# A transformer block's output projection and MLP: a scheduler's order replaced by the order of the source

## The chip, the core and the metric

The kernel runs on one core of a Trainium2 chip. A core has TensorE (PE, matrix products and transposes; its weight loads are listed apart as PEld), VectorE (DVE), ScalarE (ACT), GpSimd (POOL) and SyncE (SP), which here only issues DMA transfers. Each engine works through its own queue in order and waits on semaphores for the others. The metric is the time of one execution on the device in microseconds (us).

## The reference

One layer of a hybrid decoder block on x of 1024 rows by 1024 columns, float32. Two branches (sparse attention and a state-space scan) are merged; the part that matters here is its end:

```
merged = sigmoid(g_a) * y_a + sigmoid(g_b) * y_b
x  = x + merged @ w_out                           # 1024 x 1024
h2 = rmsnorm(x, norm_mlp_g)
x  = x + square(relu(h2 @ w_up)) @ w_down         # 1024 x 4096 and 4096 x 1024
return rmsnorm(x, norm_final_g)
```

rmsnorm(x, g) is x / sqrt(mean(x*x) + 1e-6) * g, per row.

## The kernel before

Every float32 product is made of three matmuls. An operand is split into a high part in fp32r (a cast on ScalarE) and a low part, the rest (a subtraction on VectorE or GpSimd), and high x high, low x high and high x low are added up in PSUM. So a product of a 128x512 weight block with four 128x512 blocks of the other operand is 12 matmuls.

The two products of the MLP are done by a fast scheme with seven products of half size in place of eight. With h2 cut into B11, B21 (rows 0 to 511, the two halves of the columns) and B12, B22 (rows 512 to 1023), the operands on the side of the rows are B11, B21, B22, T1 = B12 - B11, T2 = B22 - T1, T3 = B22 - B12 and T4 = B21 - T2. The weights' sums are formed per unit.

**Output projection (line 118 to 120, tile ps_o; 1033).** Two column halves, each of eight row blocks of 128 rows, 24 matmuls a block. After the second half of a row block is added to x (L1033), `norm2` norms the row: square with sum (L124), the power on GpSimd (L127), the scale and gain in one VectorE pass over 1024 columns (L977), eight transposes on PE into two PSUM banks (L983), a copy to SBUF (`hb`, L984). Rows 0 to 3 are split to B11 and B21 (L968, L969); for rows 4 to 7 the transposed blocks are subtracted (T1 in two steps from the two parts of B11, L998; T2, L1001), then split. T3 and T4 are formed later over whole operands from the split parts of others (`late_operand`, L1009 to 1014).

**Up products (L1043, tiles pa, pb, pc).** Sixteen units q; each has weights of two 128x1024 rows of w_up and seven products of 12 matmuls: two in `up_open` (B11, B21), two in `up_mid` (T2, T1), three in `up_end` (T3, B22, T4). Sums of the weights are VectorE subtractions and additions (L1070 to 1073), then a cast (L111) and a split on GpSimd (L112). Products are copied or added on ScalarE and VectorE (L1060, L1062, L1078, L1080, L1089, L1092), squared after the ReLU (L1047, L1048), summed to seven operands and written to DRAM in pairs of units (act_d, L1103 to L1105). Even units' weights are loaded by L105, odd ones by L1112, all on SyncE, where the writes are issued too.

**Down products (L1146, tile pg).** Seven operands by 16 steps of 12 matmuls. Each step takes 128x512 of the seven stored operands (loaded on SyncE, two steps at a time, L1152, two buffers) and 128x512 of w_down (loaded on ScalarE's queue by `fetch`, L1215, six steps ahead), with its own cast and split (L1164 to 1167). Then come adds to x, final norm and the write.

What sets the order: the source calls these helpers one after another, and a scheduler then lays out every engine's queue by its own estimate of when an instruction can run.

## Time and profile before

| | us |
|---|---|
| median of 3 runs (1648.69 to 1650.01) | 1648.78 |
| the profiled execution | 1651.35 |
| its span in the trace | 1649.5 |
| PE busy | 1536.3 (93%) |
| PE weight loads busy | 1281.3 (78%) |
| VectorE busy | 1038.6 (63%) |
| ScalarE busy | 744.4 (45%) |
| GpSimd busy | 471.7 (29%) |

The mean granted clock of TensorE is 0.967 of full speed. The span begins at the first instruction; what the execution takes beyond its span lies outside the trace. Busy shares are means over the whole span: the branches take the first half, the output projection lies at about 807 to 900 us, the up products follow to 1302.5, and the down products and the tail fill the rest.

### The profile page before, as it was taken

To read this page: it belongs to the slowest core of one execution; us is meant where nothing else is said; L and a number is where in the kernel's file an instruction comes from. 1 tells how busy PE (TensorE), PEld (TensorE's weight loads), DVE (VectorE), ACT (ScalarE), POOL (GpSimd) and SP (SyncE) were. 2 spreads that over 40 slices of the span, in tenths; PEclk is the share of its full clock that TensorE was granted. 3 is DMA by queue.
4 is the path that set the end of the run, shared out by engine and by line. 5 is a ranking of instruction groups with operands and counts; after the bars stand their busy time and mean duration, and the time that the engine had idled before them with its cause. 6 is when DMAs were issued, how large, how long until landed. Compare 5 with 4: busy or idle time off the path is not lost.

```text
span 1649.5 us, 22305 instructions
## 1 busy us (share of the span) xinstructions
PE 1536.3 (93%) x7890; PEld 1281.3 (78%) x7890; DVE 1038.6 (63%) x1871; ACT 744.4 (45%) x1555; POOL 471.7 (29%) x438
## 2 busy tenths in 40 slices
PE   7999999999999999999999586889899949999997
PEld 6789899888888888888888465777777738788886
DVE  7995967378889785754514883344343349755675
ACT  6344443357667675422204453444444323344453
POOL 3133544210001000000003433343324335444453
PEclk9999999999999999999999797999999979999999
DMA  6345465721132112733412123333343793344343
GB/s 225 122 117 171 117 190 149 223 75 57 60 101 64 55 49 97 254 104 127 179 51 102 64 80 111 134 140 141 141 140 115 250 327 93 90 142 151 94 130 109
DMA packets 113647, 212.12 MB, mean 129 GB/s; under 512 B 14720, under 2 KB 49536, under 8 KB 113536
## 3 DMA queue, kind: packets, MB, share of 16 engines
q1 hardware_dynamic: 104320, 193.92, 35.9%
q10 hardware_dynamic: 9216, 16.78, 2.8%
q8 instruction: 62, 1.02, 0.2%
q14 instruction: 49, 0.40, 0.1%
HBM read 140.41 MB, written 68.16 MB: 126 GB/s over the span
## 4 chain that ended last, share of the span: by engine, by line
PE 77%; DVE 10%; DMA 5%; issue 2%; ACT 2%; POOL 1%; SPq 0%; POOLq 0%; DVEq 0%; ACTq 0%
PE pg L1146 18%; PE ps_m L150 10%; PE pa L1043 9%; PE s_ps L763 4%; PE pt L804 3%; PE pc L1043 3%; PE ps_v L120 3%; PE ps_v L118 3%; PE ps_v L119 3%; PE o_ps L714 2%; PE pb L1043 2%; PE o_ps L715 2%; DMA raw<-w_up 2%; PE ps_o L120 2%; PE ps_o L118 2%
## 5 line engine op out<-in xcount | busy, mean ns | idle before, releaser
L1146 PE MATMUL pg<-w 128*128 128x512 f32 x1344 | 313.6, 394 | 23.7 <-ACT w L1164 20.8
L1146 PEld LDWEIGHTS pg<-w 128*128 128x128 f32 x1344 | 253.7, 190 | 83.4 <-ACT w L1164 21.3
L112 POOL TENSOR_TENSOR w<-raw,w 128x1024 fp32r<-128x1024 f32 (+2 forms) x75 | 179.0, 2398 | 334.1 <-ACT w L111 297.4
L150 PE MATMUL ps_m<-hT,w 128*128 128x512 f32 x768 | 215.1, 400 | 0.4 <-ACT mst L156 0.3
L1165 POOL TENSOR_TENSOR w<-raw,w 128x512 fp32r<-128x512 f32 x112 | 156.1, 1396 | 183.4 <-ACT w L1164 181.0
L1164 ACT CAST w<-raw 128x512 fp32r<-128x512 f32 x112 | 69.1, 620 | 190.7 <-POOL w L1165 111.5
L150 PEld LDWEIGHTS ps_m<-hT,w 128*128 128x128 f32 x768 | 130.6, 189 | 21.4 <-ACT mst L156 0.8
L1043 PE MATMUL pa<-T,w 128*128 128x512 f32 x576 | 140.8, 394 | 3.8 <-ACT T L1013 2.2
L1043 PEld LDWEIGHTS pa<-T,w 128*128 128x128 f32 x576 | 108.1, 188 | 30.1 <-ACT T L1013 2.6
L111 ACT CAST w<-raw 128x1024 fp32r<-128x1024 f32 (+2 forms) x98 | 95.0, 979 | 65.1 <-DMA raw<-w_out 16.6
L1167 DVE TENSOR_TENSOR w<-xy,w 128x512 fp32r<-128x512 f32 x64 | 70.9, 1118 | 65.2 <-ACT w L1166 41.5
L1043 PE MATMUL pa<-B,w 128*128 128x512 f32 x192 | 66.3, 495 | 39.4 <-ACT w L111 27.3
L769 ACT ACTIVATE p<-s_ps,sst 128x640 f32<-128x640 f32 (+7 forms) x128 | 90.2, 708 | 23.5 <-PE pt L804 13.4
L1043 PEld LDWEIGHTS pa<-B,w 128*128 128x128 f32 x192 | 45.8, 243 | 57.0 <-ACT w L111 30.3
L127 POOL TENSOR_TENSOR rstd<-ss,neghalf 128x1 f32<-128x1 f32 x16 | 9.3, 580 | 281.2 <-DVE ss L125 281.2
L763 PE MATMUL s_ps<-kT,qT 128*128 128x512 f32 (+3 forms) x384 | 85.9, 337 | 0.3
L804 PE MATMUL pt<-ident,p 128*128 128x128 f32 x528 | 83.8, 275 | 2.1 <-DVE pl__5079 L708 1.0
L1167 DVE TENSOR_TENSOR w<-z,w 128x512 fp32r<-128x512 f32 x48 | 60.6, 1268 | 39.3 <-ACT w L1166 39.3
L766 DVE CUSTOM_DVE_ANT_0 s_ps<-s_ps,cmask 128x256 f32<-128x256 f32 (+7 forms) x96 | 63.9, 677 | 19.9 <-PE s_ps L763 19.4
L119 PE MATMUL ps_a<-w,hT 128*128 128x256 f32 (+1 forms) x256 | 74.7, 292 | 0.0
L118 PE MATMUL ps_a<-w,hT 128*128 128x256 f32 (+1 forms) x256 | 74.5, 291 | 0.0
L120 PE MATMUL ps_a<-w,hT 128*128 128x256 f32 (+1 forms) x256 | 73.9, 289 | 0.0
(1423 smaller groups left out, 3458.2 us busy)
## 6 DMA issues: line engine op xcount, KB each, us to landing
raw<-act_d SPq DMA_DIRECT2D x56, 512.0 KB
raw<-w_up SPq DMA_DIRECT2D x35, 512.0 KB
act_d<-ts SPq DMA_DIRECT2D x16, 1024.0 KB
raw<-w_mg SPq DMA_DIRECT2D x16, 512.0 KB
mg_d<-mst SPq DMA_DIRECT2D x32, 256.0 KB
act_d<-e SPq DMA_DIRECT2D x16, 512.0 KB
xy<-w_down ACTq DMA_DIRECT2D x32, 256.0 KB
z<-w_down ACTq DMA_DIRECT2D x32, 256.0 KB
```

What stands on the lines that cost most here:

```text
L111: (hi or A.copy)(w[:, 0, :], raw)
L112: (lo or V.tensor_tensor)(w[:, 1, :], raw, f32(w[:, 0, :]), op=ALU.subtract)
L118: T.matmul(ps, lhsT=wh, rhs=xh, start=first and i == 0, stop=False)
L119: T.matmul(ps, lhsT=wl, rhs=xh, start=False, stop=False)
L120: T.matmul(ps, lhsT=wh, rhs=xl, start=False, stop=last and i == n - 1)
L150: m = T.matmul(ps, lhsT=w[:, e, ks], rhs=hT[k][:, r, hs], start=k == 0 and i == 0, stop=k == KD - 1 and i == 2)
L763: T.matmul(s_ps[:, o:o + hi - lo], lhsT=qT[:, 2 + hp * 2 + j, :], rhs=kT[g, br, hf][:, e, lo - hf * 512:hi - hf * 512], start=e == 0, stop ...
L804: T.transpose(pt[:, i, j, :], c[hp, br][j][:, (i0 + i) * P:(i0 + i + 1) * P], ident)
L1043: T.matmul(ps, lhsT=w[:, e, ks], rhs=x[:, k], start=first and k + i == 0, stop=k == 3 and i == 2, skip_group_check=not first)
L1146: T.matmul(ps[b], lhsT=w[:, 0, e, bs], rhs=w[:, 1, r], start=first and q + i == 0, stop=q == 15 and i == 2, skip_group_check=not first)
L1165: G.tensor_tensor(w[:, 0, 1], raw[:, q % 2], f32(w[:, 0, 0]), op=ALU.subtract)
L1167: V.tensor_tensor(w[:, 1, 1], t, f32(w[:, 1, 0]), op=ALU.subtract)
```

## The change

From the output projection on the scheduler is off (`tc.manual_schedule()`): each engine's queue has the order of the source. The source is rewritten as a pipeline. For a unit q of the up stage the products come as p1, p2, p6, p5, p7, p3, p4, and between them stand the preparations of unit q+1 (`prep_open`, `prep_s`, `prep_a`, `prep_b`, `prep_c`); the weight loads of unit q+2 are issued ahead of the writes of unit q. In the down stage `prep(u)` does step u's casts, splits and differences three steps ahead, issues one load of the activations for every two steps and one `fetch` of w_down four steps ahead (AHEAD was 6). The first three steps are prepared between the last products of the up stage.

The norm is cut into parts (`norm_a`, `norm_b`, `norm_d3`, `norm_split`) that run at different row blocks. The scale is a ScalarE pass, the gain a VectorE one. The differences T1, T2 and T3 are formed on the normed rows, in SBUF, ahead of the transposes; every operand then has transposes of its own (112 instead of 64), and the splits read PSUM without a copy. T4 is formed block by block from B21 and T2's transposed rows.

```diff
-ND3, E4, S4B, NOPEN, AHEAD = 5, 5, 2, 3, 6
+ND3, E4, S4B, AHEAD = 5, 5, 2, 4
...
+        st3.enter_context(tc.manual_schedule())
+        c1, c2 = slice(0, 512), slice(512, 1024)
...
-        def split_to(name, js, src, lo=None):
+        def blk(b):
+            return slice(b % 4 * P, b % 4 * P + P)
+
+        def transposed(src, bank="p"):
+            pt = dps.tile([P, 4, P], F32, name="pt", tag="p", bufs=2) if bank == "p" else \
+                dps.tile([P, 4, P], F32, name="pt", tag="d")
+            for k in range(4):
+                T.transpose(pt[:, k, :], src[:, k * P:(k + 1) * P], ident)
+            return pt
+
+        def split_to(name, b, pt):
             h, l = ops_[name]
-            A.copy(h[:, :, js], src)
-            (lo or V).tensor_tensor(l[:, :, js], src, f32(h[:, :, js]), op=ALU.subtract)
...
-        xr = []
-
-        def norm2(b):
-            js = slice(b % 4 * P, b % 4 * P + P)
-            xs = e4("xs")
-            rstd = rms_rows(ep, xr[b], xs.rearrange("p (e d) -> p e d", e=2))
-            V.scalar_tensor_tensor(xs, xr[b], rstd, gm, op0=ALU.mult, op1=ALU.mult)
+            A.copy(h[:, :, blk(b)], pt)
+            V.tensor_tensor(l[:, :, blk(b)], pt, f32(h[:, :, blk(b)]), op=ALU.subtract)
+
+        xr, xl, xs, rst = [], [], {}, {}
+
+        def norm_a(b, ps):
+            V.tensor_tensor(xr[b][:, c2], xr[b][:, c2], ps, op=ALU.add)
             nc.sync.dma_start(x_d[b], xr[b])
-            hb = e4("hb", (P, 2, 4, P))
-            for kh in range(2):
-                pt = dps.tile([P, 4, P], F32, name="pt", tag="p", bufs=2)
-                for k in range(4):
-                    T.transpose(pt[:, k, :], xs[:, (kh * 4 + k) * P:(kh * 4 + k + 1) * P], ident)
-                A.copy(hb[:, kh], pt)
+            xs[b] = e4("xs")
+            rst[b] = rms_rows(ep, xr[b], xs[b].rearrange("p (e d) -> p e d", e=2))
+
+        def norm_b(b):
+            x = xs[b]
+            A.activation(x, xr[b], AF.Copy, scale=rst[b])
             if b < 4:
-                if b == 0:
-                    op2("B11", mpool, "m")
-                    op2("B21", mpool, "m")
-                split_to("B11", js, hb[:, 0])
-                split_to("B21", js, hb[:, 1], G)
+                if b % 2 == 0:
+                    xl.append(s4("xl", (P, 2, 512)))
+                V.tensor_tensor(xl[b // 2][:, b % 2], x[:, c1], gm[:, c1], op=ALU.mult)
+                V.tensor_tensor(x[:, c2], x[:, c2], gm[:, c2], op=ALU.mult)
                 return
+            d1 = xl[b // 2 - 2][:, b % 2]
+            V.tensor_tensor(x, x, gm, op=ALU.mult)
+            V.tensor_tensor(d1, x[:, c1], d1, op=ALU.subtract)
+            V.tensor_tensor(xr[b][:, c2], x[:, c2], d1, op=ALU.subtract)
+
+        def norm_d3(b):
+            V.tensor_tensor(xr[b][:, c1], xs[b][:, c2], xs[b][:, c1], op=ALU.subtract)
+
+        def norm_split(b):
+            if b == 0:
+                op2("B11", mpool, "m")
+                op2("B21", mpool, "m")
             if b == 4:
                 op2("B22", oppool, "opT")
                 op2("T1", oppool, "opT")
                 op2("T2", mpool, "m")
-            t1 = hb[:, 0]
-            for e in range(2):
-                V.tensor_tensor(t1, t1, f32(ops_["B11"][e][:, :, js]), op=ALU.subtract)
-            split_to("B22", js, hb[:, 1], G)
-            split_to("T1", js, t1)
-            V.tensor_tensor(hb[:, 1], hb[:, 1], t1, op=ALU.subtract)
-            split_to("T2", js, hb[:, 1])
...
-        def late_operand(name, x, y):
-            op2(name, oppool, "opT")
-            for k in range(4):
-                (xh, xl), (yh, yl) = ([f32(o[:, k]) for o in ops_[n]] for n in (x, y))
-                t = mstp.tile([P, 512], F32, name="tt", tag="mst")
-                V.tensor_tensor(t, xh, yh, op=ALU.subtract)
-                V.tensor_tensor(t, t, xl, op=ALU.add)
-                V.tensor_tensor(t, t, yl, op=ALU.subtract)
-                h, l = ops_[name]
-                A.copy(h[:, k], t)
-                V.tensor_tensor(l[:, k], t, f32(h[:, k]), op=ALU.subtract)
...
+            lo = xl[b // 2 % 2][:, b % 2]
+            if b < 4:
+                pts = [("B11", transposed(lo)), ("B21", transposed(xs[b][:, c2]))]
+            else:
+                pts = [("T1", transposed(lo)), ("T2", transposed(xr[b][:, c2])), ("B22", transposed(xs[b][:, c2], "d"))]
+            for name, pt in pts:
+                split_to(name, b, pt)
...
+        tts = []
+
+        def t3_chunk(b):
+            if b == 4:
+                op2("T3", oppool, "opT")
+            split_to("T3", b, transposed(xr[b][:, c1]))
+
+        def t4_chunk(b):
+            if b == 4:
+                op2("T4", oppool, "opT")
+            if b % 2 == 0:
+                tts.append(s4("tt", (P, 2, 512)))
+            pt = transposed(xr[b][:, c2])
+            t = tts[-1][:, b % 2].rearrange("p (k j) -> p k j", k=4)
+            h, l = ops_["B21"]
+            V.tensor_tensor(t, f32(h[:, :, blk(b)]), pt, op=ALU.subtract)
+            V.tensor_tensor(t, t, f32(l[:, :, blk(b)]), op=ALU.add)
+            split_to("T4", b, t)
...
+        def cast(parts, n, halves=False):
+
+            w = wpool.tile([P, 2, S], F32R, name="w", tag="w", bufs=nbuf[1])
+            for i, x in enumerate(parts):
+                A.copy(w[:, 0, i * n:i * n + n], x)
+                G.tensor_tensor(w[:, 1, i * n:i * n + n], x, f32(w[:, 0, i * n:i * n + n]), op=ALU.subtract)
+            return w
+
+        def prep_open(q, raw0, parts=1):
+            u = us[q] = Pair()
+            u.wo = cast([raw0[:, i * S // parts:(i + 1) * S // parts] for i in range(parts)], S // parts)
+
+        def prep_s(q):
+
+            u = us[q]
+            u.sa = s4("sa", (P, S))
+            V.tensor_tensor(u.sa[:, c2], u.a21, u.a22, op=ALU.add)
+            V.tensor_tensor(u.sa[:, c1], u.sa[:, c2], u.raw0[:, c1], op=ALU.subtract)
+
+        def prep_a(q):
+            u = us[q]
+            u.wa = cast([u.sa], S)
+
+            V.tensor_tensor(u.raw0[:, c1], u.raw0[:, c1], u.a21, op=ALU.subtract)
+            V.tensor_tensor(u.raw0[:, c2], u.raw0[:, c2], u.sa[:, c1], op=ALU.subtract)
+
+        def prep_b(q):
...
+        for b in range(NB):
+            ps = wout(1, b, ws1)
+            norm_a(b, ps)
+            if b > 1:
+                norm_split(b - 2)
+            if b == 6:
+                prep_open(0, r[0], 2)
+            if b < 7:
+                norm_b(b)
+                if b > 3:
+                    norm_d3(b)
+        prep_open(1, r[1])
+        p1(0)
+        norm_b(7)
+        norm_split(6)
+        p2(0)
+        p2_square(0)
+        r2 = load(wpool, a["w_up"][4], S)
+        prep_open(2, r2)
+        p1(1)
...
+        prep_s(0)
+        prep_a(0)
+        norm_split(7)
+        p2(1)
...
+        p1(2)
+        t3_chunk(4)
+        t3_chunk(5)
+        p2(2)
...
+        p6(0)
+        t4_chunk(4)
+        t4_chunk(5)
...
+        for q in range(1, 16):
+            n = q + 1
+            if q + 2 < 16 and q > 0:
+                up_raw(q + 2)
...
+            if q >= 3:
+                p1(q)
+                p2(q)
+            if n < 16 and n > 2:
+                prep_open(n, raws[n][0])
...
+            if n < 16:
+                prep_s(n)
+            p6(q)
+            p5(q)
+            if n < 16:
+                prep_a(n)
+            else:
+                for u in range(4):
+                    fetch(u)
+            p7(q)
+            if n == 16:
+                prep(0)
+            p3(q)
+            if n < 16:
+                prep_b(n)
+            p3_square(q)
...
+            p4(q)
...
+            sums(q)
...
+        def prep(u):
...
+            n, q = divmod(u, 16)
+            raw = araw[u // 2][:, u % 2]
+            w = held[u] = wpool.tile([P, 2, 2, 512], F32R, name="w", tag="w", bufs=nbuf[1])
+            t = right(n, q)
+            A.copy(w[:, 0, 0], raw)
+            G.tensor_tensor(w[:, 0, 1], raw, f32(w[:, 0, 0]), op=ALU.subtract)
+            A.copy(w[:, 1, 0], t)
+            V.tensor_tensor(w[:, 1, 1], t, f32(w[:, 1, 0]), op=ALU.subtract)
+            if u % 2:
+                load_acts(u // 2 + 2)
+            fetch(u + AHEAD)
...
+            for q in range(16):
+                prep(16 * n + q + 3)
+                if later:
+                    later.pop(0)()
...
+                for b in range(4):
+                    mms(ps[b], first, q, held[16 * n + q], b)
```

SyncE in the up stage, before (e1, e2 and ts are a unit's results, act_d their place in DRAM, raw and raw2 the weights of an even and an odd unit):

```order
L1104 DMA act_d3_164<-e2_10678 128x512
L1112 DMA raw2_10764<-w_up 128x1024 x2
L1103 DMA act_d3_164<-e1_10641 128x2x512
L1105 DMA act_d3_164<-ts_10756 128x4x512
L1104 DMA act_d3_164<-e2_10809 128x512
L105 DMA raw_11158<-w_up 128x1024
L105 DMA raw_11160<-w_up 128x1024
L1103 DMA act_d3_164<-e1_10772 128x2x512
L1105 DMA act_d3_164<-ts_10887 128x4x512
```

and of the changed kernel, the same stretch of the queue:

```order
L1169 DMA raw2_10555<-w_up 128x1024 x2
L1158 DMA act_d2_163<-e1_10559 128x2x512
L1159 DMA act_d2_163<-e2_10595 128x512
L1160 DMA act_d2_163<-ts_10678 128x4x512
L105 DMA raw_10686<-w_up 128x1024
L105 DMA raw_10688<-w_up 128x1024
L1158 DMA act_d3_164<-e1_10691 128x2x512
L1159 DMA act_d3_164<-e2_10727 128x512
L1160 DMA act_d3_164<-ts_10810 128x4x512
```

The write of e2 stood ahead of the odd units' weight loads; now the loads stand ahead of a unit's three writes, which come together.

ScalarE at the start of the down stage, before (xy and z hold w_down, raw the stored operands, w a step's split tile):

```order
L1215 DMA xy<-w_down 128x512 x3
L1164 CAST w<-raw 128x512
L1166 CAST w<-xy 128x512
L1215 DMA xy<-w_down 128x512 x3
L1166 CAST w<-xy 128x512
L1215 DMA xy<-w_down 128x512 x8
L1215 DMA z<-w_down 128x512 x9
L1164 CAST w<-raw 128x512 x2
L1166 CAST w<-xy 128x512 x2
```

and changed (e_11871 and e_11901 are the last up unit's results):

```order
L1209 DMA xy<-w_down 128x512 x4
L1062 ACTIVATE e_11901<-e_11901 128x512
L1063 ACTIVATE e_11901<-e_11901 128x512
L1230 CAST w<-raw 128x512
L1232 CAST w<-xy 128x512
L1209 DMA xy<-w_down 128x512
L1062 ACTIVATE e_11901<-e_11901 128x512
L1063 ACTIVATE e_11901<-e_11901 128x512
L1230 CAST w<-raw 128x512
L1232 CAST w<-xy 128x512
L1209 DMA xy<-w_down 128x512
```

Seventeen loads in a row became four, and then one behind each step's two casts, among the last unit's squares.

VectorE where rows 4 to 7 are normed, before (hb is a transposed normed row, xs a normed row, T and B the split operands, e an up product):

```order
L977 SCALAR_TENSOR_TENSOR xs<-x_9272,rstd,gm 128x1024
L1001 TENSOR_TENSOR hb<-hb 128x512
L969 TENSOR_TENSOR T_9607<-hb,T_9606 128x4x128
L998 TENSOR_TENSOR hb<-hb,B_9394 128x512
L998 TENSOR_TENSOR hb<-hb,B_9395 128x512
L125 TENSOR_SCALAR ss<-ss 128x1
L977 SCALAR_TENSOR_TENSOR xs<-x_9272,rstd,gm 128x1024
L969 TENSOR_TENSOR T_9605<-hb,T_9604 128x4x128
L1001 TENSOR_TENSOR hb<-hb 128x512
L998 TENSOR_TENSOR hb<-hb,B_9394 128x512
L1062 TENSOR_TENSOR e_9792<-e_9792,pb 128x512
```

and changed (x_9117 holds a row of x and later its differences, xl the first halves of the normed rows):

```order
L988 TENSOR_TENSOR x_9117<-x_9117,ps_o 128x512
L125 TENSOR_SCALAR ss<-ss 128x1
L983 TENSOR_TENSOR T_9675<-pt,T_9674 128x4x128
L983 TENSOR_TENSOR T_9677<-pt,T_9676 128x4x128
L983 TENSOR_TENSOR B_9673<-pt,B_9672 128x4x128
L1003 TENSOR_TENSOR xs<-xs,gm 128x1024
L1004 TENSOR_TENSOR xl<-xs,xl 128x512
L1005 TENSOR_TENSOR x_9117<-xs,xl 128x512
L1008 TENSOR_TENSOR x_9117<-xs 128x512
L988 TENSOR_TENSOR x_9117<-x_9117,ps_o 128x512
```

Subtractions on transposed blocks (L998, L1001) became subtractions on rows (L1004, L1005, L1008), and the splits (L983) read the transposes' PSUM bank.

## Rows read from the trace of the kernel before

**Rows 1.** Tile ps_o: count, ns min/median/max, first and last start (us).

```profile
L120 PE MATMUL ps_o<-w,mT x128: 389/392/480, 807.8 to 899.6; 128*128 128x512 f32 x128
```

**Rows 2.** Stretches: length, busy PE, PEld, DVE, ACT, POOL; clock, DMA share, GB/s.

```profile
900.00:1002.00 102.00, 66.35 (x284) 52.63 (x282) 77.47 (x92) 46.99 (x78) 38.46 (x19) 0.84 0.33 116
1002.00:1302.50 300.50, 274.24 (x1093) 216.93 (x1094) 114.67 (x141) 129.88 (x197) 120.22 (x55) 0.92 0.36 126
1302.50:1341.50 39.00, 17.65 (x74) 13.15 (x72) 11.62 (x14) 7.01 (x13) 4.55 (x5) 0.77 1.01 376
1341.50:1440.00 98.50, 96.17 (x397) 75.85 (x398) 86.12 (x86) 39.55 (x70) 54.47 (x36) 0.97 0.39 123
1440.00:1600.00 160.00, 160.00 (x705) 132.28 (x704) 97.62 (x96) 71.40 (x132) 77.15 (x61) 1.00 0.41 124
```

**Rows 3.** Chain of waits, two units of the up stage: start, us, what.

```profile
1218.24 2.75 PE pc L1043 x12
1221.00 2.80 PE pa L1043 x12
1223.88 0.70 DVE e L1089
...
1225.92 0.33 SPq L1104
...
1226.36 4.14 DMA raw<-w_up
...
1231.68 2.36 POOL w L112
...
1234.08 4.81 PE pa L1043 x11
```

**Rows 4.** SyncE's waits, 1000 to 1300: us in total, times, longest.

```profile
SPq L1104 <- ACT e L1048: 193.9, 12, 30.5
```

**Rows 5.** ScalarE's instructions one by one, 1321 to 1341: start, us, what.

```profile
1321.63 13.71 ACTq L1215 DMA_DIRECT2D xy<-w_down  x8
1335.78 4.93 ACTq L1215 DMA_DIRECT2D z<-w_down  x9
1340.75 0.62 ACT L1164 CAST w<-raw 128x512 fp32r<-128x512 f32 x1 [19.65 <-DMA z<-w_down]
```

**Rows 6.** VectorE's instructions one by one, from 1441.

```profile
1441.39 1.31 DVE L1167 TENSOR_TENSOR w<-xy,w 128x512 fp32r<-128x512 f32 x1 [1.42 <-ACT w L1166]
1444.12 1.30 DVE L1167 TENSOR_TENSOR w<-xy,w 128x512 fp32r<-128x512 f32 x1 [1.42 <-ACT w L1166]
```

**Rows 7.** Chain of waits, a row's transposes among the output projection.

```profile
866.37 0.87 PE pt L983 x8
```

**Rows 8.** Groups of instructions, 840 to 1000: busy us, mean ns, idle before.

```profile
L977 DVE SCALAR_TENSOR_TENSOR xs<-x,rstd,gm 128x1024 f32<-128x1024 f32 x8 | 14.4, 1802 | 4.1 <-POOL rstd L127 4.1
L124 ACT ACTIVATE xs<-x 128x1024 f32<-128x1024 f32 x8 | 8.5, 1062 | 34.8 <-DVE x L1033 34.8
L968 ACT CAST B<-hb 128x512 fp32r<-128x512 f32 x12 | 7.1, 628 | 0.0
```

**Rows 9.** TensorE's waits, 899.9 to 1005: us in total, times, longest.

```profile
PE pt L983 <- DVE xs L977: 17.6, 2, 11.0
PE pa L1043 <- ACT w L111: 14.9, 2, 13.6
```

**Rows 10.** Groups of instructions, 1000 to 1280.

```profile
L112 POOL TENSOR_TENSOR w<-raw,w 128x1024 fp32r<-128x1024 f32 x25 | 61.7, 2470 | 153.2 <-ACT w L111 116.5 <-DMA act_d<-e 36.7
L1070 DVE TENSOR_TENSOR sa<-raw 128x512 f32<-128x512 f32 x13 | 21.3, 1675 | 8.5 <-DMA raw<-w_up 8.2
L1072 DVE TENSOR_TENSOR raw<-raw 128x512 f32<-128x512 f32 x12 | 8.2, 685 | 19.4 <-POOL w L112 19.4
```

**Rows 11.** Line 1146, the down products.

```profile
L1146 PE MATMUL pg<-w x1344: 387/389/794, 1302.4 to 1639.3; 128*128 128x512 f32 x192
```

**Rows 12.** Chain of waits, start of the down stage.

```profile
1320.71 10.75 DMA y<-x_d
```

More of the change, by code (lines that the diff above doesn't have):

```diff
@@ L1097, in up_end, with p3, p3_square, p4 @@
+        def p3(q):
+            u = us[q]
+            prod(u.pc, u.wb[:, :, c2], "B22", False)
+            V.tensor_tensor(u.e2[:, 0], u.e2[:, 0], u.pc, op=ALU.add)
+        def p3_square(q):
+            square(us[q].e2[:, 0])
+        def p4(q):
+            u = us[q]
+            prod(u.pa, u.wc[:, :, 0:512], "T4", False)
+            square(u.e1[:, 1], u.pa)
+        def sums(q):
+            u = us[q]
+            e1, e2 = u.e1, u.e2
             t = mpool.tile([P, 4, 512], F32, name="ts", tag="m")
@@ L1105, in up_end @@
             nc.sync.dma_start(d[:, 3:7, q % 2], t)
+        raws = {}
         def up_raw(q):
@@ L1182, in hybrid_block @@
[L1182 to L1198 removed]
+                raws[q] = t[:, 0], t[:, 1]
+            else:
+                raws[q] = [load(wpool, a["w_up"][2 * q + i], S) for i in range(2)]
@@ new lines, in hybrid_block @@
+        gm = e4("gm")
+        ws0, ws1 = [], []
+        for j in range(4):
+            ws0.append(weights(mpool, a["w_out"][0, j], S, tag="m", bufs=8))
+        for b in range(NB):
+            if b % 2 == 0:
+                x2 = mpool.tile([P, 2, S], F32, name="x2", tag="m")
+            xr.append(x2[:, b % 2, :])
+            nc.sync.dma_start(xr[b], a["x"][b * P:(b + 1) * P, :])
+        nc.sync.dma_start(gm, a["g_mlp"])
+        for b in range(NB):
+            ps = wout(0, b, ws0)
+            if b < 4:
+                ws1.append(weights(wpool, a["w_out"][1, b], S))
+            V.tensor_tensor(xr[b][:, c1], xr[b][:, c1], ps, op=ALU.add)
@@ new lines, in hybrid_block @@
+        r = [load(wpool, a["w_up"][2 * q], S) for q in range(2)]
+        a21, a22 = (mstp.tile([P, 512], F32, name="mst", tag="mst") for _ in range(2))
+        nc.sync.dma_start(a21, a["w_up"][1][:, c1])
+        nc.sync.dma_start(a22, a["w_up"][1][:, c2])
+        for b in range(NB):
+            ps = wout(1, b, ws1)
[8 more added lines that the diff above has]
+                    norm_d3(b)
@@ new lines, in hybrid_block, with mms, add @@
+        y = []
+        gfin = e4("gfin")
+        later = []
+        def mms(ps, first, q, w, b):
+            bs = slice(b * P, b * P + P)
+            for i, (e, r) in enumerate(((0, 0), (1, 0), (0, 1))):
+                T.matmul(ps, lhsT=w[:, 0, e, bs], rhs=w[:, 1, r], start=first and q + i == 0,
+                         stop=q == 15 and i == 2, skip_group_check=not first)
+        def add(b, cs, ps):
+            V.tensor_tensor(y[b][:, cs], y[b][:, cs], ps, op=ALU.add)
+        groups = ([dps.tile([P, 512], F32, name="pg0", tag="p", bufs=2), dps.tile([P, 512], F32, name="pg1", tag="p", bufs=2),
+                   mps.tile([P, 512], F32, name="pg2", tag="d"), acc("pg3")], [acc(f"pg{4 + i}") for i in range(4)])
@@ new lines, in hybrid_block @@
+        for n in range(7):
+            ps, first, (r, cs) = groups[n % 2], n in (0, 1, 5), DST[n]
+            if n in (2, 3):
+                first = False
+            for q in range(16):
+                prep(16 * n + q + 3)
+                if later:
+                    later.pop(0)()
+                if n == 3 and q == 8:
+                    nc.sync.dma_start(gfin, a["g_fin"])
+                if n < 2 and q % 4 == 2:
+                    if len(y) % 2 == 0:
+                        y2 = mpool.tile([P, 2, S], F32, name="y2", tag="m")
+                        y.extend((y2[:, 0], y2[:, 1]))
+                    i = n * 4 + q // 4
+                    nc.sync.dma_start(y[i], x_d[i])
+                if n == 5 and q % 4 == 2:
+                    pre(q // 4)
+                if n == 5 and q % 4 == 3:
+                    pre(4 + q // 4)
+                if n == 6 and q >= 12:
+                    continue
+                for b in range(4):
+                    mms(ps[b], first, q, held[16 * n + q], b)
+            for b in range(4):
+                if n < 6:
+                    later.append(lambda b=b, cs=cs, p=ps[b], r=r: add(r * 4 + b, cs, p))
+                    if n == 5:
+                        later.append(lambda b=b, r=r: final(r * 4 + b))
+                else:
+                    for q in range(12, 16):
+                        mms(ps[b], first, q, held[16 * n + q], b)
+                    add(4 + b, cs, ps[b])
+                    final(4 + b)
```

260 lines of the change are left out of this document (110 added, 150 removed).

## The prediction

> **What bounds the kernel now.** I read the busy times by stage first, for where TensorE (PE) stops, then the chain of waits inside those stages for what ends each stop, then SyncE's queue and the single instructions for prices. Up to 900 us PE is full, and the change begins at the output projection, whose last matmul starts at 899.6 [rows 1]. From there to the end four stages lose time [rows 2]. 900 to 1002, where the rows are normed and the first products begin: PE is busy 66 of 102 us. 1002 to 1302.5, the up products: 1093 matmuls in 300.5 us at a mean granted clock of 0.92. 1302.5 to 1341.5, the start of the down stage: 74 matmuls in 39 us, while the DMA engines are full at 376 GB/s. 1341.5 to 1440: 397 matmuls in 98.5 us. Only 1440 to 1600 is full, at clock 1.00.
>
> The up stage loses its time once per two units. The chain at 1223.88 shows it [rows 3]: the VectorE add of the T3 product, two ScalarE passes of the squared ReLU (to 1225.9), then SyncE writes that half to DRAM, and only behind this write does it issue the two loads of the next odd unit's weights. The load lands 4.14 us later, the cast follows, GpSimd splits it in 2.36, and PE restarts at 1234.08. SyncE stood 193.9 us, 12 times, before that write [rows 4]. The first eleven matmuls after the stop take 4.81 us; twelve take 2.75 or 2.80 in full flow [rows 3], so about 2.3 us more go to the lower of the two clock levels (1.2 GHz) after the stop.
>
> The down stage starts badly for a reason of order: ScalarE holds eight, then nine issues of weight loads ahead of one cast, and that cast ends PE's wait at 1341 [rows 5].
>
> **The sum, stage by stage.** Prices: a product is 12 matmuls, 2.78 us (mean of 2.75 and 2.80 [rows 3]); a down step (12 matmuls) is 2.73 us, the spacing of VectorE's splits at 1441 [rows 6]; a 128x128 transpose is 0.87 / 8 = 0.109 us [rows 7]. I write the profiled execution as 1651.35 us, 1.85 above its span.
>
> Up to the last output projection matmul: 44 transposes instead of 32 stand ahead of it, +1.3 us.
>
> Start-up, from there to the end of the first unit's seventh product: PE's own work is 11 products (30.6) and 68 transposes (7.4). The waits have no row, since the new order never ran. From the queues: a normed row of the second half runs on VectorE and ScalarE as add 0.69, square 1.06, two or three casts of an earlier row's transposes (0.63 each, they stand ahead on ScalarE), scale (taken like the square, 1.06), gain at most 1.80, and three 512-wide differences of 0.69 [rows 8, 10]. That is 7.9 to 8.6 us, against 6.4 to 6.9 of PE work for the same row (24 matmuls and 8 or 12 transposes). Four such rows, one of which also casts the first unit's weights, leave VectorE about 6 us late when PE ends the last one. PE then meets this at three places: the transposes of rows 6 and 7, whose two PSUM banks come free only when VectorE has split the rows before (4 us); the third opening product, whose load waits for a buffer, then lands, is cast and split (2 us); and the T4 product, whose last block needs the last transposed difference (4 us). With two restarts at the lower clock of 2 us each I take 14. The bounds are 0, if the five PSUM banks hide it all, and 37, what PE waits at this place now (the two largest are 17.6 and 14.9, of five [rows 9]). I choose 14 since the late operands, which now cost VectorE 24 512-wide subtractions or additions over whole operands, become blocks between products. Start-up: 52 us.
>
> The other 101 products: 280.8 us. What hides the rest: each unit's weights are cast and split during the unit before. Cast and split are about 1.06 and 2.47 us [rows 8, 10] and stand at least four products ahead of their use. A PSUM bank is read (0.63 to 0.69) while another product of 2.78 runs, since the order p1, p2, p6, p5, p7, p3, p4 never uses one bank twice running. Loads for unit q+2 stand ahead of the writes of unit q on SyncE and are used a unit (19.5 us) later, against the 4.14 us landing. Per unit GpSimd has three splits of 2.47 and a half one, 9 us; ScalarE some 14 instructions of 0.6 to 1.06, 12 us; VectorE ten of 0.69 to 1.68 [rows 10], at most 17. All fit into 19.5. If the loads were still late, each pair would go on losing some 6 to 7 us.
>
> So the stretch from 900.0 to 1302.5 (402.5 us) becomes 1.3 + 52.0 + 280.8 = 334.1, which is 68.4 less.
>
> Down: 112 x 2.73 = 305.8. One weight load is issued behind each step's casts, four steps ahead, instead of seventeen in a row. The same bytes are asked for over two operands: per two steps 0.5 MB of activations, 0.5 of weights, 0.25 of x, 1.3 MB in 5.5 us or 240 GB/s; 376 was moved [rows 2]. At the seam the first three steps are prepared between the last products on queues that also hold their squares; I take 2 us (0 to 5). The third operand forms two differences per step on VectorE, which with its split come to some 3.0 us a step (two of 0.69, one lengthened to 1.68 [rows 10]); 1341.5 to 1440 loses 98.5 - 397 x 2.73 / 12 = 8 us now. Three steps in hand cover part of it, and again in the last operand, where four final norms go between; 5 us for both. Sum 312.8 against the 337.2 from 1302.5 to PE's end at 1639.7 (the last start, 1639.3, and 0.39 [rows 11]), 24.4 less. The tail (9.8 us) keeps its adds, norms and writes: 0.
>
> 1651.35 - 68.4 - 24.4 = 1558.5. The profiled execution lies 2.6 above the median of 1648.78, so I forecast 1556 us, 5.6% less.
>
> **One page against a row.** A 512-wide subtraction of two SBUF tiles takes 0.69 us on VectorE; L1070, the same shape, has a mean of 1.68, in a stretch where GpSimd's splits run [rows 10]. The Trainium skill (SBUF — State Buffer, "SBUF: two separate sides") has an exclusive lock here: a VectorE instruction with two SBUF inputs and a GpSimd one that reads SBUF do not share, the later one blocks for the whole instruction. The trace agrees in size (1 us more for one such instruction); no run here shows the lock itself. By that rule the row differences, now SBUF to SBUF, would wait for the first units' splits and the sum would be that of rival (a), 1579, where the plain 0.69 gives 1556.
>
> **Rivals.** (a) The start-up stays long. It has 28 VectorE instructions with two SBUF inputs (four gains, twelve differences, four T4 sums, eight for the first weights). If most cost 1.0 us more, as L1070 against 0.69, and VectorE is already late, the start-up grows by some 23 us, to the 37 of waits that stand there now: 1579. For it: VectorE is busy 77 of 102 us there [rows 2]. Against: the new order has fewer passes. (b) Two load slots pace the first two down operands. A slot is held from issue until GpSimd has split both halves; two slots serve four steps, 10.9 us, and 4.6 of them go to the second half's step (2.73), its cast (0.63) and its split (half of 2.47); so from a landing of 6.3 us on they decide. At the 10.75 us that a load took at 1320 [rows 12], a step is (10.75 + 4.6) / 4 = 3.84 us, 1.1 x 32 = 35 more: 1591. Against: that row is from full DMA engines; 240 GB/s is well below. (c) Nothing of the 14 us waits shows: 1542. (d) The other side: queues in the order of the source stop each other at every step. A late cast holds ScalarE, thus the next copy, thus PE. There are 213 products and steps after the start-up; with 0.44 us lost at each (half of it the lower clock) the 93 us are gone, and beyond that the kernel is slower, say 1665. For it: a queue now waits where a scheduler could have put other work ahead. Against: 2.1 us or more of cover at each bank and a unit at each weight.
>
> **Chances.** Forecast 0.62 (its own 1545 to 1570), (a) 0.18, (b) 0.09, (c) 0.07, (d) 0.03; 0.01 for an even result. The range of 1535 to 1590 reaches below (c) by the product price (2.73 for 2.78 is 5 us) and, above, as good as to (b). A measurement of this kernel tells about 0.2% (3.3 us) from no change: faster by more 0.96, within 0.01, slower 0.03.
>
> **What would show it.** In the new profile: no SyncE wait of some 190 us on ScalarE before an act_d write that has loads behind it; PE full at clock 1.00 from about 955 to 1235, with a product every 2.78 us; PE's remaining idle time between 900 and 955, ended by VectorE and GpSimd; no full DMA stretch at the seam; the first down matmul near 1237 and the last near 1547. Wrong would be a short PE stop in each unit (d), loads of act_d that end ScalarE's waits in the first two down operands (b), or the first unit's end later than 965 (a).

## The result and the profile after

The changed kernel takes 1576.35 us (median of 4 runs, 1574.98 to 1578.97), the kernel before 1649.39 in the same comparison: a ratio of 0.9555, 95% interval 0.9536 to 0.9574, so 73 us or 4.5% less. The forecast was 1556 us with a range of 1535 to 1590. The profiled execution took 1575.71 us (span 1572.8), 17.2 more than the 1558.5 of the sum.

Stage by stage, between the starts of the first and last matmuls (before: [rows 1, 11]; after: last of tile ps_o at 900.3, first and last down matmul in the row below):

| us | before | forecast | after |
|---|---|---|---|
| last output projection matmul | 899.6 | +1.3 | +0.7 |
| from there to the first down matmul | 402.8 | 332.8 | 332.6 |
| of it the first unit, to the end of its T4 product | | 52.0 | 51.1 |
| of it the other 101 products | | 280.8 | 281.3 |
| down, to PE's end | 337.3 | 312.8 | 330.0 |
| tail | 9.8 | 9.8 | 9.9 |

The down products in the changed kernel, count, ns (min/median/max), first and last start:

```profile
L1362 PE MATMUL pg<-w x1344: 387/389/795, 1232.9 to 1562.5; 128*128 128x512 f32 x192
```

Busy time by stretch (columns as in [rows 2]), cut where the stages of the sum end:

```profile
900.50:951.60 51.10, 43.47 (x201) 35.31 (x200) 37.07 (x51) 26.11 (x43) 18.02 (x9) 0.87 0.14 52
951.60:1232.90 281.30, 281.30 (x1213) 227.91 (x1213) 160.89 (x158) 144.78 (x216) 122.55 (x57) 1.00 0.45 155
1232.90:1262.00 29.10, 26.69 (x112) 20.52 (x111) 17.88 (x15) 13.90 (x26) 15.69 (x11) 1.00 0.80 267
...
1320.00:1375.00 55.00, 54.37 (x219) 38.72 (x219) 53.73 (x56) 22.54 (x40) 25.59 (x19) 1.00 0.50 158
...
1520.00:1562.90 42.90, 34.83 (x123) 24.09 (x121) 30.92 (x41) 12.74 (x26) 12.98 (x13) 0.88 0.28 93
```

PE is full at clock 1.00 for the 281.3 us of the other 101 products, where before it had 274 of 300 and a clock of 0.92 [rows 2]. Down loses time in three stretches. At 2.73 us for 12 matmuls, 1232.9 to 1262 is 29.1 - 112 x 2.73 / 12 = 3.6 us too long, 1320 to 1375 (the third operand) 5.2, and 1520 to 1562.9 (the last) 14.9 us. In the last, PE stands idle for 8.1 of these us (34.83 of 42.9 busy); the rest lies in matmuls that take longer, at a mean granted clock of 0.88. In the third operand PE counts as busy nearly throughout (54.37 of 55), and the loss shows in its weight loads, which wait a little at every step. The waits of PE, in us in all, times, longest (L1362 is a down product, L1058 an up product, L977 a transpose; L982 and L983 are cast and split of a transposed block):

```profile
PE pg L1362 <- ACT w L1232: 8.3, 6, 2.1
PE pa L1058 <- ACT T L982: 3.7, 1, 3.7
PE pt L977 <- DVE T L983: 3.0, 1, 3.0
PE pg L1362 <- DVE w L1233: 1.8, 1, 1.8
PE pa L1058 <- DVE T L983: 0.9, 1, 0.9
```

SyncE still waits long for squares before the first write of a unit:

```profile
SPq L1158 <- ACT e L1063: 193.3, 14, 15.9
```

That is as much as before [rows 4], and the loads of a later unit still stand behind it. It costs nothing now, since those loads are used a unit later.

**Where down lost its 17 us.** VectorE, ScalarE, GpSimd and PE's weight loads (PEld) in the third operand, instruction by instruction (start, us, what, idle before). L1230 is ScalarE's cast of the stored operand and L1231 GpSimd's split of it, L1217 and L1218 are the two differences, L1232 is ScalarE's cast of the difference, L1233 its split, L1366 an add of PSUM to y:

```profile
1330.00 1.32 POOL L1231 TENSOR_TENSOR w<-raw,w 128x512 fp32r<-128x512 f32 x1 [1.80 <-ACT w L1230]
1330.10 1.77 DVE L1217 TENSOR_TENSOR xy<-z,xy 128x512 f32<-128x512 f32 x1
1330.23 2.15 PEld L1362 LDWEIGHTS pg<-w 128*128 128x128 f32 x10 [0.44 <-DVE w L1233]
1331.91 0.62 ACT L1232 CAST w<-xy 128x512 fp32r<-128x512 f32 x1 [1.98 <-DVE xy L1217]
...
1332.58 0.30 PEld L1362 LDWEIGHTS pg<-w 128*128 128x128 f32 x2 [0.20 <-ACT w L1232]
1332.62 0.69 DVE L1233 TENSOR_TENSOR w<-xy,w 128x512 fp32r<-128x512 f32 x1
1333.13 1.33 POOL L1231 TENSOR_TENSOR w<-raw,w 128x512 fp32r<-128x512 f32 x1 [1.80 <-ACT w L1230]
1333.23 0.68 DVE L1366 TENSOR_TENSOR y<-y,pg 128x512 f32<-128x512 f32 x1
1333.36 2.15 PEld L1362 LDWEIGHTS pg<-w 128*128 128x128 f32 x10 [0.49 <-DVE w L1233]
1333.83 1.18 DVE L1217 TENSOR_TENSOR xy<-z,xy 128x512 f32<-128x512 f32 x1
```

One kind of instruction has two durations. L1217, with both inputs in SBUF, starts 0.1 us after GpSimd's split and takes 1.77 us; at 1333.83, 0.7 us into the split, it takes 1.18. Both end 0.55 us after the split does (1331.32 and 1334.46). The add from PSUM at 1333.23 runs beside the split in 0.68. In the second operand the difference (L1215 there) sometimes starts first, and then it is the split that is long:

```profile
1289.67 0.68 DVE L1215 TENSOR_TENSOR xy<-xy 128x512 f32<-128x512 f32 x1
1289.73 1.77 POOL L1231 TENSOR_TENSOR w<-raw,w 128x512 fp32r<-128x512 f32 x1 [1.13 <-ACT w L1230]
```

Below, "the lock" is this: of the two instructions, the one that starts later lasts until after the other's end. The rule of the Trainium skill (SBUF — State Buffer, "SBUF: two separate sides") on a VectorE instruction with two SBUF inputs and a GpSimd one that reads SBUF is what these rows show: the later one waits for the whole of the other. And since VectorE's queue is in the order of the source, the next difference comes only after the split of the step, which waits for ScalarE's cast, which waits for the difference. Here a step takes 3.13 us (GpSimd's splits start at 1330.00 and 1333.13) against PE's 2.73. So it is in the whole third operand and in the second half of the second one: VectorE begins the second operand's steps at 1272.33 and the third's at 1320.69, 48.4 us for 16 steps where PE takes 43.7, and that uses up most of the three steps in hand. In the last operand the steps ahead of the norms take some 2.75 us and the last four some 3.07; what is lost there comes mostly from the norms.

The last operand adds the norms, every second step:

```profile
1523.67 0.68 DVE L1366 TENSOR_TENSOR y<-y,pg 128x512 f32<-128x512 f32 x1
1524.27 1.20 DVE L1220 TENSOR_TENSOR z<-z,xy 128x512 f32<-128x512 f32 x1
...
1527.26 0.55 POOL L1384 TENSOR_TENSOR rstd<-sq,neghalf 128x1 f32<-128x1 f32 x1 [2.34 <-DVE sq L1382]
1527.77 1.30 POOL L1231 TENSOR_TENSOR w<-raw,w 128x512 fp32r<-128x512 f32 x1
1527.84 2.44 DVE L1386 SCALAR_TENSOR_TENSOR y<-y,rstd,gfin 128x512 f32<-128x512 f32 x2 [0.67 <-POOL rstd L1384]
...
1532.18 0.68 DVE L1366 TENSOR_TENSOR y<-y,pg 128x512 f32<-128x512 f32 x1
```

The add hides the lock (the difference behind it takes 1.20), but VectorE waits 0.67 us for GpSimd's power, and the two scales take 2.44 us beside the next split. Two steps last 8.51 us (1523.67 to 1532.18, where the next add starts), 3.05 more than PE's 5.46. There are four such pairs, of 8.30 to 8.52 us.

### The profile page after: what moved, and what is told of

The parts are those of the page before. It is cut to its first block, busy times and chain, and to the rows that moved or that the text cites. A ratio compares the mean times of both kernels' runs of the same rounds, so it can differ in the third digit from the quotient of the medians.

```text
span 1572.8 us, 22363 instructions
## 1 busy us (share of the span) xinstructions
PE 1526.6 (97%) x7938; PEld 1273.7 (81%) x7938; DVE 1057.5 (67%) x1867; ACT 746.4 (47%) x1548; POOL 443.1 (28%) x431
## 5 line engine op out<-in xcount | busy, mean ns | idle before, releaser
L1362 PE MATMUL pg<-w 128*128 128x512 f32 x1344 | 318.9, 396 | 11.1 <-ACT w L1232 8.3
L1362 PEld LDWEIGHTS pg<-w 128*128 128x128 f32 x1344 | 251.5, 190 | 78.3 <-ACT w L1232 14.1
L1231 POOL TENSOR_TENSOR w<-raw,w 128x512 fp32r<-128x512 f32 x112 | 151.5, 1357 | 172.7 <-ACT w L1230 172.7
L1058 PE MATMUL pa<-T,w 128*128 128x512 f32 x576 | 143.8, 399 | 4.6 <-ACT T L982 3.7
L1058 PEld LDWEIGHTS pa<-T,w 128*128 128x128 f32 x576 | 109.4, 191 | 31.2 <-ACT T L982 4.1
L1075 POOL TENSOR_TENSOR w<-raw,w 128x1024 fp32r<-128x1024 f32 (+1 forms) x48 | 100.5, 2095 | 109.9 <-ACT w L1074 108.2
L1230 ACT CAST w<-raw 128x512 fp32r<-128x512 f32 x112 | 69.2, 618 | 103.7 <-POOL w L1231 60.2
L112 POOL TENSOR_TENSOR w<-raw,w 128x1024 fp32r<-128x1024 f32 (+1 forms) x27 | 71.1, 2638 | 162.4 <-ACT w L111 162.4
L1233 DVE TENSOR_TENSOR w<-xy,w 128x512 fp32r<-128x512 f32 x64 | 69.3, 1092 | 49.8 <-ACT w L1232 30.0
L1233 DVE TENSOR_TENSOR w<-z,w 128x512 fp32r<-128x512 f32 x48 | 56.7, 1187 | 45.5 <-ACT w L1232 43.6
L763 PEld LDWEIGHTS s_ps<-kT,qT 128*128 128x128 f32 x384 | 63.6, 189 | 11.5 <-ACT p L769 1.3
L804 PEld LDWEIGHTS pt<-ident,p 128*128 128x128 f32 x528 | 62.4, 140 | 12.3 <-PE s_ps L763 1.3
```

The costliest lines, as they stand in the source:

```text
L763: T.matmul(s_ps[:, o:o + hi - lo], lhsT=qT[:, 2 + hp * 2 + j, :], rhs=kT[g, br, hf][:, e, lo - hf * 512:hi - hf * 512], start=e == 0, stop ...
L804: T.transpose(pt[:, i, j, :], c[hp, br][j][:, (i0 + i) * P:(i0 + i + 1) * P], ident)
L1058: T.matmul(ps, lhsT=w[:, e, ks], rhs=x[:, k], start=first and k + i == 0, stop=k == 3 and i == 2, skip_group_check=not first)
L1075: G.tensor_tensor(w[:, 1, i * n:i * n + n], x, f32(w[:, 0, i * n:i * n + n]), op=ALU.subtract)
L1231: G.tensor_tensor(w[:, 0, 1], raw, f32(w[:, 0, 0]), op=ALU.subtract)
L1233: V.tensor_tensor(w[:, 1, 1], t, f32(w[:, 1, 0]), op=ALU.subtract)
```

## The experiments

Twelve kernels, medians of 4 runs, each with its ratio to the kernel before in the same comparison. The first theory was that the fixed order of the queues makes the gain. Its rival was the rewritten source. The up stretch is from the last output projection matmul to the first down matmul, down from there to PE's end.

| | us | ratio to before (95%) | up | down |
|---|---|---|---|---|
| changed source, scheduler on | 1588.39 | 0.9637 (0.9621 to 0.9652) | 333.1 | 343.4 |
| old source, fixed order | 2134.84 | 1.2945 (1.2925 to 1.2966) | 800.7 | 364.3 |
| changed, loads behind writes | 1638.25 | 0.9936 (0.9918 to 0.9953) | 394.4 | 333.1 |
| before, row differences alone | 1661.85 | 1.0083 (1.0066 to 1.0100) | 388.8 | 338.9 |
| before, loads ahead of writes | 1610.00 | 0.9758 (0.9729 to 0.9788) | 356.0 | 343.4 |
| changed, loads in a row | 1585.16 | 0.9608 (0.9592 to 0.9624) | 332.7 | 338.9 |
| changed, split on VectorE | 1559.90 | 0.9453 (0.9430 to 0.9476) | 333.2 | 313.7 |
| changed, difference a step ahead | 1568.95 | 0.9509 (0.9487 to 0.9531) | 333.1 | 322.9 |
| changed, norms in pieces | 1570.12 | 0.9513 (0.9487 to 0.9539) | 332.9 | 326.8 |
| changed, start-up moved | 1575.21 | 0.9547 (0.9525 to 0.9570) | 332.2 | 333.1 |
| split on VectorE and norms in pieces | 1552.88 | 0.9415 (0.9394 to 0.9436) | 332.9 | 309.8 |
| the same, row 5's split earlier | 1553.09 | 0.9414 (0.9392 to 0.9436) | 332.5 | 309.3 |

### Where the gain came from

**The scheduler back on the changed source.**

```diff
-        st3.enter_context(tc.manual_schedule())
```

> The changed source, but the scheduler lays out the queues again (the one line that turns it off is taken out). Theory: the gain is in the fixed order of the queues; the scheduler puts writes ahead of loads and weight loads in a row again, so the time goes back most of the way, 1620 to 1655 us. Rival: the gain is in the rewritten source (fewer passes, smaller pieces), and the scheduler keeps it, 1570 to 1585.

The theory fell. 1588.39 us keeps 60 of the 73 us, and the up stretch is 333.1 against 332.6. What the fixed order itself gives is at the start of the down stage; PE's largest wait there with the scheduler on, and ScalarE's queue ahead of it:

```profile
PE pg L1361 <- ACT w L1229: 25.9, 1, 25.9
```

```profile
1261.05 9.93 ACTq L1208 DMA_DIRECT2D xy<-w_down  x8
1271.77 12.27 ACTq L1208 DMA_DIRECT2D z<-w_down  x16
1284.08 1.14 ACT L1229 CAST w<-raw 128x512 fp32r<-128x512 f32 x2 [23.44 <-DMA z<-w_down]
```

Twenty-four loads stand ahead of two casts, as in [rows 5]. But in the last operand this kernel loses nothing (59.5 of 59.5 us busy from 1520). VectorE there:

```profile
1520.81 1.30 DVE L1232 TENSOR_TENSOR w<-z,w 128x512 fp32r<-128x512 f32 x1 [0.69 <-ACT w L1231]
1522.14 0.69 DVE L1219 TENSOR_TENSOR z<-z,xy 128x512 f32<-128x512 f32 x1
```

The split L1232 takes the lock's delay (1.30), and the next difference follows it at once, not behind the next cast. So the fixed order is worth some 26 us at one end of the stage and costs some 15 at the other.

**The old source in a fixed order.** The same line, put into the kernel before at the output projection.

> The old source with the scheduler off from the output projection on, so that the queues follow a source that isn't written as a pipeline. Theory: the pipeline in the source is what the order needs; without it the load, cast and split of a unit stand behind the products of the unit before on ScalarE and VectorE, some 10 us or more lost in each of 16 units: 1750 to 1900 us. Rival: any fixed order is better than the scheduler's, 1580 to 1630.

2134.84 us, further than the theory went: PE waits 266.5 us for ScalarE's casts of weights (48 times) and 83.9 for GpSimd's splits in the up stage. In these two kernels a fixed order was as good as the source that it followed.

**Loads behind the writes, in the changed kernel.**

```diff
         for q in range(1, 16):
-            if q + 2 < 16 and q > 0:
-                up_raw(q + 2)
...
             sums(q)
+            if q + 2 < 16:
+                up_raw(q + 2)
```

> Changed kernel, but in the up stage the loads of unit q+2 are issued behind the writes of unit q. Theory: that queue order on SyncE is what the up stage gained; a unit's loads then land some 7 us after the unit before it began, where its cast is due at about 5.6, so each of 13 units loses 1 to 3 us: 1590 to 1615 us. Rival: with the load used a unit after its issue the place in the queue is covered, 1575 to 1580.

It was right in sign, but the price was 62 us. ScalarE and PE's wait:

```profile
1110.43 0.59 ACT L1106 COPY e<-pa 128x512 f32<-128x512 f32 x1 [1.01 <-PE pa L1058]
1118.51 1.04 ACT L1074 CAST w<-raw 128x1024 fp32r<-128x1024 f32 x1 [7.48 <-DMA raw<-w_up]
...
1120.65 0.57 ACT L1121 COPY e<-pa 128x512 f32<-128x512 f32 x1
```

```profile
PE pa L1058 <- ACT e L1121: 37.3, 13, 5.9
```

The cast L1074 waits 7.48 us for its load, and the copy L1121, which PE needs to reuse a PSUM bank, is queued behind it. PE loses up to 5.9 us at a time and then runs on the lower clock (mean 0.92 from 970 to 1230).

**The same move alone, in the kernel before** (scheduler on).

```diff
             if q > 1:
-                raws = up_raw(q)
+                raws = nxt
...
+            if 0 < q < 15:
+                nxt = up_raw(q + 1)
             up_end(q, us[q])
```

> The kernel before (scheduler on), with one edit: in the up stage the source asks for the loads of unit q+1 ahead of the writes of unit q, not behind them. Theory: moving the loads alone doesn't help, since their buffers come free only when the unit before has cast its weights, and the old source casts a unit's weights in the unit itself; the loads stay late: 1635 to 1650 us. Rival: the place of the loads alone was what cost the up stage 60 us: 1590 to 1620 us.

My theory, that the loads can't move without the pipeline, was wrong. This one edit takes 39.5 us off: the up stretch is 46.8 shorter, down 6.1 longer. The up stage is full:

```profile
900.00:1002.00 102.00, 69.02 (x286) 54.16 (x284) 78.68 (x93) 47.12 (x78) 39.87 (x20) 0.83 0.32 113
1002.00:1260.00 258.00, 256.88 (x1098) 208.31 (x1099) 125.12 (x142) 129.44 (x195) 118.90 (x54) 0.99 0.42 147
```

256.9 of 258 us busy after 1002, while the start-up (69 of 102 us, 66 in [rows 2]) stays as it was, and so does the stop at the start of the down stage (25.0 us behind one cast). So 46.8 of the 70 us gained in the up stretch are the place of the loads, and about 23, by difference, are the start-up. The edit the other way round, in the changed kernel above, agrees in sign.

**Row differences alone, in the kernel before** (its `norm2` and `late_operand` replaced by those of the change, with the old calls).

> The kernel before with the row differences alone: T1, T2, T3 formed on normed rows, T4 from B21 and the transposed T2 rows, splits read PSUM; scheduler and up and down stages as before. Theory: this part is worth little by itself, 1640 to 1655 us, since the scheduler's order of the start-up stays. Rival: fewer VectorE passes are what shortened the start-up (37 us of waits went to 7.6), 1615 to 1630.

Slower by 13 us. The up stretch gains 14, but the last output projection matmul comes at 925.9, 26 later: PE waits for the gain pass ahead of transposes (15.5 us, three times). In the changed source, where the rows' parts stand at other places, the start-up takes 51 us, and some 52 with the scheduler on (333.1 less 281.3). Which of the two does how much was not separated.

**Loads in a row, in the changed kernel.** Fourteen fetches between the third and fourth step's casts.

```diff
-            fetch(u + AHEAD)
+            fetch(u + (AHEAD if u < 3 else AHEAD + 13))
...
             sums(q)
+            if n == 16:
+                for u in range(7, 20):
+                    fetch(u)
```

> Changed kernel, but at the start of the down stage fourteen w_down loads stand in a row on ScalarE's queue between the casts of the third and the fourth step (one stands there now); from then on loads are seventeen steps ahead. Theory (the stop at the start of the down stage, in the kernel before and with the scheduler on, comes from loads in a row ahead of a cast): TensorE stops again for 15 to 26 us behind that cast, 1588 to 1602 us. Rival (the three steps in hand cover it, and the old stop came from the DMA engines being full in any order): 1576 to 1582 us.

The mechanism is shown, but a third as large as the 25.9 us above: 8.8 us more, between both forecasts. ScalarE, then PE:

```profile
1237.44 11.73 ACTq L1209 DMA_DIRECT2D xy<-w_down  x11
1249.22 0.62 ACT L1230 CAST w<-raw 128x512 fp32r<-128x512 f32 x1 [11.56 <-DMA xy<-w_down]
...
1252.99 0.33 ACTq L1209 DMA_DIRECT2D xy<-w_down  x1
```

```profile
1233.39 8.82 PE L1365 MATMUL pg<-w 128*128 128x512 f32 x36
1250.41 49.90 PE L1365 MATMUL pg<-w 128*128 128x512 f32 x207 [8.20 <-ACT w L1232]
```

Eleven of the issues hold ScalarE for 11.73 us, and PE stops 8.20 us behind the cast. The three steps in hand cover the rest, and this row is the shorter one (14 issues against 24). Why an issue takes 1.07 us in such a row, where a single one takes 0.33, no run separates; the DMA engines were 0.89 busy from 1233.4 to 1262.

### Where the forecast missed

**The split of the stored operand on VectorE.**

```diff
-            G.tensor_tensor(w[:, 0, 1], raw, f32(w[:, 0, 0]), op=ALU.subtract)
+            (V if n in (1, 2, 6) else G).tensor_tensor(w[:, 0, 1], raw, f32(w[:, 0, 0]), op=ALU.subtract)
```

> Changed kernel, but in the second, third and last operand of the down stage the low part of the stored operand is formed on VectorE, not on GpSimd: one 512-wide subtraction more per step on the engine that is late there. Theory (a two-SBUF-input VectorE instruction and GpSimd's split shut each other out, so the difference lasts 1.78 where it needs 0.69, and the ScalarE cast behind it waits too): with GpSimd idle the difference takes 0.69, a step 2.1 to 2.8 us in place of 3.13, and the time falls to 1558 to 1568 us. Rival (VectorE simply has a long queue in order, difference, wait for the cast, split): 0.69 us more in each of 48 steps, 1590 to 1610 us.

The engine that was late got one instruction more per step, and the kernel became 16 us faster. VectorE in the third operand:

```profile
1322.82 0.68 DVE L1217 TENSOR_TENSOR xy<-z,xy 128x512 f32<-128x512 f32 x1
1323.54 0.69 DVE L1218 TENSOR_TENSOR xy<-xy 128x512 f32<-128x512 f32 x1
1324.33 0.69 DVE L1231 TENSOR_TENSOR w<-raw,w 128x512 fp32r<-128x512 f32 x1
1324.93 0.68 DVE L1233 TENSOR_TENSOR w<-xy,w 128x512 fp32r<-128x512 f32 x1
1325.54 0.69 DVE L1217 TENSOR_TENSOR xy<-z,xy 128x512 f32<-128x512 f32 x1
```

Every instruction takes 0.68 or 0.69 us and a step 2.72 (1322.82 to 1325.54), where it took 3.13. The down stage:

```profile
L1362 PE MATMUL pg<-w x1344: 387/389/794, 1235.1 to 1548.4; 128*128 128x512 f32 x192
```

From 1235.1 to 1548.8 it takes 313.7 us, where the prediction had 312.8. Of the 17.2 us that the down stage missed, 16.3 are gone: the shared lock is the cause of most of the miss.

**The difference a step ahead.**

```diff
-            t = right(n, q)
+            t = rights[u]
...
             V.tensor_tensor(w[:, 1, 1], t, f32(w[:, 1, 0]), op=ALU.subtract)
+            if u + 1 < 112:
+                rights[u + 1] = right(*divmod(u + 1, 16))
```

> Changed kernel, but the difference of step u+1 stands on VectorE right behind the split of step u, a step earlier than now. Theory (what is lost in the third and the last operand is a loop in order: difference, cast on ScalarE, split, and only then the next difference): the loop opens as the cast finds its input ready, VectorE needs 2.0 to 2.7 us a step, and of the 22 us lost in these two operands some 15 go: 1556 to 1567 us. Rival (it is the sum of VectorE's and GpSimd's work under the shared lock that is too long, in any order): 1571 to 1578 us.

7.4 us, half of what I expected and between both. The loop is opened, but the lock moves to whatever VectorE does beside the split; now both scales meet one:

```profile
1522.38 0.68 DVE L1220 TENSOR_TENSOR z<-z,xy 128x512 f32<-128x512 f32 x1
...
1524.04 3.48 DVE L1392 SCALAR_TENSOR_TENSOR y<-y,rstd,gfin 128x512 f32<-128x512 f32 x2 [0.66 <-POOL rstd L1390]
1527.44 0.68 DVE L1237 TENSOR_TENSOR w<-z,w 128x512 fp32r<-128x512 f32 x1
```

The scales' 3.48 us were 2.44, and in the last steps the differences still take 1.77 to 1.80.

**The norms in pieces.** Square, power and each half scale at different steps; in the tail a row's scales behind the next row's add.

```diff
-                        later.append(lambda b=b, r=r: final(r * 4 + b))
...
+                    later[b + 1] = later[b + 1] + [lambda b=b: final_a(b)]
+                    later[b + 2] = later[b + 2] + [lambda b=b: final_b(b)]
...
+                        later[4 + 2 * b + i] = later[4 + 2 * b + i] + [lambda b=b, s=s: final_c(b, s)]
```

> Changed kernel, but the final norm of a row is cut into square, power and two half scales that go between different steps (and between different rows in the tail). Theory (in the last operand both the loop of difference, cast and split and the scales under GpSimd's split are late; the round trip to GpSimd's power is only a part): a pair of steps falls from 8.5 to some 7 us, 1566 to 1573 us. Rival (the round trip of the norm, 3.06 us in each of four pairs, is all of the loss): 1560 to 1565 us.

As the theory had it: 6.2 us. Of these about 2.4 are the tail (7.5 us from PE's end to the span's end, 9.9 in the changed kernel). With GpSimd's split beside it a half scale takes 1.76 to 1.80 us, so the step stays long.

**The start-up.**

```diff
+            if b == 7:
+                norm_split(5)
             norm_a(b, ps)
-            if b > 1:
+            if 1 < b < 7:
                 norm_split(b - 2)
...
         t4_chunk(6)
+        t4_split(5)
         half_raws(1)
         prep_s(1)
-        p7(0)
-        prep_a(1)
+        t4_split(6)
         t4_chunk(7)
+        prep_a(1)
+        t4_split(7)
+        p7(0)
```

> Changed kernel, but in the start-up T4's differences are issued a block ahead of its casts and splits, the last block ahead of unit 1's preparations, and the split of row block 5 ahead of row block 7's norm. Theory (TensorE's waits there, 3.0 us on row 6's transposes and 4.6 us on T4, come from what stands ahead on VectorE): 4 to 6 us less with the lower clock behind them, 1570 to 1573 us. Rival (the work that is moved back is then what TensorE waits for): 1575 to 1578 us.

The rival was right: 1.1 us less is within the spread of the runs. PE's waits:

```profile
PE pa L1063 <- DVE e L1137: 4.3, 1, 4.3
PE pa L1063 <- POOL w L1080: 3.7, 2, 2.1
```

The 3.0 us before row 6 are 1.0 in all, but PE then waits 3.7 for the splits of the opening weights, and the 4.6 of T4 became 4.3 for the add of the T3 product.

**Both edits.**

> Changed kernel with two edits together: stored operands' low parts on VectorE in the second, third and last operand, and the final norms cut into pieces. Theory: they meet different waits (the shared lock, and the round trip of the norms and the tail's chain of 3.9 us a row), so the second still gains 3 to 5 us on top of the 1559.9: 1554 to 1558 us. Rival: with the lock gone nothing waits for the norms, 1559 to 1561 us.

1552.88 us, more than the theory asked (7.0 below the split alone), and the best with the next, which moves row 5's split on top:

> As the run with both edits, and the split of row block 5 stands ahead of row block 7's norm. Theory: TensorE's wait of 3.0 us before row 6's transposes, with the lower clock behind it, falls to about 1 us: 2 to 4 us less than without, 1551 to 1555 us. Rival: the wait moves to the next product, no change within 1 us.

1553.09: no change, the wait moved to the next product.

## Why the prediction came out as it did

The 1576.35 us lie inside the stated range, but outside the forecast's own 1545 to 1570. One term of the sum carries the miss.

- **What bounds the kernel: right.** The place of the loads on SyncE [rows 3, 4] was 46.8 us of the up stretch by itself, in the old kernel; the lower clock went with the stops.
- **Start-up, 52.0: right in size (51.1), by places in part.** Row 6's transposes waited 3.0 (forecast 4), T4 4.6 (4), the third opening product not at all (2). That is 7.6 in all where the sum had 10, and PE's busy time is 5.5 above its own work of 38.0, at a clock of 0.87, where it had 4 for two restarts: that 14 fits so well is in part luck. Rival (a) is out there: eleven of the twelve differences among the rows took 0.69 and one 1.31; the four gains took 1.22 to 2.09. GpSimd was busy 18.0 of the 51.1 us.
- **Other products, 280.8: right (281.3),** and the loads behind the writes show that their place carries it (394.4 against 332.6 us of up stretch). That the order is fixed is not needed: the scheduler on the same source has it too.
- **Seam (the start of the down stage), 2: right (2.3 us of waits,** 3.6 with the slower pace around them). Rival (b) was felt: casts waited for stored operands up to 7.7 us (20.9 in all), and the three steps in hand took it; its 35 us did not come.
- **"Third and last operand, 5 for both": wrong, 20.1.** This term is the miss: 5.2 in the third, 14.9 in the last. The prediction put the long difference (1.68) into the third operand and set three steps in hand against it. It left it out of the second, which uses up those steps, and of the last; and it took the norms as added work, not as a wait in order (difference, cast, split, power, scale) of 8.5 us for two steps. The rule of the Trainium skill (SBUF — State Buffer, "SBUF: two separate sides") holds, and so does the prediction's 1 us more per instruction (1.77 against 0.69), but the prediction looked for them in the start-up. The 1579 of rival (a) is near the measured time by chance.
- **Tail, 0: right (+0.1).** It was not at its floor, though: the norms in pieces make it 2.4 shorter.
- **"No SyncE wait of some 190 us ahead of loads": wrong.** It stays at 193.3 and is harmless; what counts is when the loads behind it are due.

Not settled: how the 23 us of the start-up divide between row differences and their places, and how much of the scheduler's own order at the start of the down stage would go with another rule for loads; the latter was not tried.

## What to carry to other kernels

A long wait in a DMA queue matters by the due time of what stands behind it: move the loads first, alone, before rewriting the order. Turning the scheduler off paid here only where the source was already a pipeline (1576.35 us against 1588.39; with the old source 2134.84 against 1649.39), and what it then lost was in chains through several engines, which had to be cut into pieces by hand. Before an engine that is late is given less work, look whether another engine's instruction is what lengthens its own.
